# A Strassen-tiled decoder kernel: when the first weight sums of a wide phase are loaded, and in which order its side work runs

## The chip, the cores and the metric

The kernel runs on one core of one Trainium2 chip. The metric is the device time of one execution in microseconds; a profile of one execution gives the time of each instruction.

## The reference

Two decoder layers on 256 tokens of width 2048, in fp32. Each layer has a token mixer (layer 0: dilated sliding-window attention; layer 1: stick-breaking attention; both beside a cross-attention into 256 memory tokens) and a gated MLP. The change is in the MLP alone:

```python
def _conv_ffn(h, w_up, w_conv, b_conv, w_down):
    u = h @ w_up                                  # (256 x 2048) @ (2048 x 11264)
    gate, val = jnp.split(u, 2, axis=-1)          # 5632 columns each
    gp = jnp.pad(gate, ((0, 0), (CONV_WIDTH - 1, 0), (0, 0)))
    acc = b_conv + gp[:, CONV_WIDTH - 1:CONV_WIDTH - 1 + S] * w_conv[CONV_WIDTH - 1]
    for j in range(CONV_WIDTH - 1):
        acc = acc + gp[:, j:j + S] * w_conv[j]
    return (jax.nn.silu(acc) * val) @ w_down
```

## The kernel before, in words

Matmuls keep fp32's precision by splitting each operand into a rounded high part and the rest (`split`, L592 to L594: a cast on ScalarE at L593, a difference on VectorE at L594) and adding three products, high by high, low by high, high by low (`mm3`, L127).

**The groups.** The 5632 columns of the MLP are 11 groups of 512. Odd groups (1, 3, 5, 7, 9) are wide: `wide` (L596) forms a group's gate and value columns by a Strassen scheme, seven products in place of eight, in eight units over the 2048 inputs. Even groups are narrow: eight tiles of 128 columns (two pairs, each with gate and value), each a plain product over the 2048 inputs. Narrow group 0 runs alone (`narrow`, L801). The others run beside a wide group (`beside`, L815): each of the eight units of a wide phase has one narrow tile at its side (`ws_beside`, L151), so that a phase makes wide group g and narrow group g + 1. Behind a phase `downs` (L737) multiplies two finished groups by their rows of w_down, in four chunks of 512 output columns, two chunks at a time, eight pieces of weights in all; each chunk's partial result is copied out (L748) and stored or added to memory by a DMA from POOL (L750, L752). So each layer has five wide phases: the first behind narrow(0), four behind downs.

**A unit.** On PE, in this order: the first half of the side tile (16 matmuls, L156), wide products 1, 2, 3 (L127), the side tile's second half, wide products 7, 5, 6, 4. Products 1 to 3 use plain weights, 7 and 5 the first sum d, 6 and 4 the second sum e. The sum d of two quarter blocks comes by DMA: a load on SP (L628) and an accumulating DMA on POOL (L629), written for the first two units ahead of the phase (`first_sums`, L625) and for unit u + 2 within unit u. VectorE then adds twice (L636, L637) for e. Both sums are split into one set of buffers, `forms` (named x in the profile), which the next unit may overwrite only when products 7, 5, 6, 4 are done.

**The side tile.** It takes one of four "s" banks of PSUM; the other three are held by wide products, so the next side tile can begin only when the last one has been copied (L168, ScalarE) and added (L169, VectorE) out of its bank. Its weights are split in two halves into "whi" and "wlo", four buffers each, shared with the plain weights.

**The pair's steps.** When a pair of side tiles has its gate, the gate is scaled (`gate`, L797), convolved (ScalarE's first tap with the bias at L773, VectorE's other taps at L763, SiLU at L765), and when the value is there multiplied by it (`keep`) and split. These are put in a list (`behind_this`), and `catch_up` takes one entry from it at two places of each unit. The sums of h that products 3, 5, 6, 7 need are made eight in number by `sums_of_h` (L568): five during narrow(0), and the last three from the same list, in the first phase of a layer (L582 to L587, then a split at L285, L286).

**What sets the order.** A planner places instructions by the program's order as far as buffers and its estimates of readiness allow, and each engine then runs its own list in order. Inside a phase the compute instructions are pinned (`pin`): on each engine they stand in the program's order. DMAs are not pinned, nor is anything ahead of the phase's loop or in the downs. "sh" is a pool of 11 buffers for the activations (two for each group), output copies, d and e; "raw" has three buffers for weights as loaded.

Of the kernel before, what the change touches and what calls it, by code (L numbers as in the profile page):

```python
# [10 lines left out]
F32 = mybir.dt.float32  # L11
F32R = mybir.dt.float32r
# [5 lines left out]
P = 128  # L18
# [27 lines left out]
class Body:  # L46
# [103 lines left out]

    def ws_beside(self, out, src, h, done=None):  # L151

        parts = self.piece(src)
        yield
        b = self.bank("s")
        mm = lambda *o, **k: self.pin(self.nc.tensor.matmul(*o, **k))  # L156
# [11 lines left out]
        self.pin(self.nc.scalar.copy(out, b[:, S:]))  # L168
        self.pin(self.nc.vector.tensor_add(out, b[:, 0:S], out))  # L169
        if done:  # L170
            done()
# [396 lines left out]
    def sums_of_h(self, h):  # L568

        nc, pin = self.nc, self.pin
        s = self.sb.tile([P, KT // 2, 4, 2, P], F32R, name="h1", tag="h1", bufs=1)

        def less(out, x, y):

            pin(nc.vector.scalar_tensor_tensor(out, x, -1.0, y, op0=ALU.mult, op1=ALU.subtract))

        def make(i):
            a, d = self.pairtile(), self.pairtile().rearrange("p a (b t) -> p (a b) t", b=2)  # L580
            hh = h[2][:, 2 * i:2 * i + 2, :, :].bitcast(F32)
            pin(nc.vector.tensor_add(a, hh[:, :, 0, :], hh[:, :, 1, :]))  # L582
# [10 lines left out]
        self.pin(self.nc.scalar.copy(hi, of))  # L593
        self.pin(self.nc.vector.tensor_sub(lo, of, hi.bitcast(F32)))  # L594

    def wide(self, src, h, s, forms, r, beside):  # L596

# [24 lines left out]
            nc.sync.dma_start(raw[:, :1536], src[u][:, :1536])  # L622
            return raw

        def first_sums(u):  # L625

            d = self.sh([P, 1024])
            nc.sync.dma_start(d, src[u][:, 512:1536])  # L628
            nc.gpsimd.dma_start(d.rearrange("p (a n) -> p a n", a=2),  # L629
                                src[u][:, 1536:].unsqueeze(1).to_broadcast([P, 2, 512]), accum_op=ALU.add)  # L630
            return d

        def sums(d, raw):

            e = self.sh([P, 1024])
# [14 lines left out]
            for of, parts in zip(t, summed):  # L650
                self.split(*parts, of)

        ahead = [first_sums(0), first_sums(1)]
        raw = load(0)
        t = sums(ahead.pop(0), raw)
        split_sums(t)
        b = beside[0]()
        next(b)
        f = plain(raw)
        self.pinned = True  # L660
        for u in range(n):
            more = u + 1 < n
            next(b)
            if u:
                split_sums(t)
            self.catch_up()
            fa, fb = f
            product(1, u, fa, 1)
            product(2, u, fa, 0)
            product(3, u, fb, 0)  # L670
            if more:
                raw = load(u + 1)
                if u + 2 < n:
                    ahead.append(first_sums(u + 2))
# [32 lines left out]
    def ffn(self, layer, h, each, filler=None, done=None, late=None):  # L707
# [20 lines left out]
        s, make = self.sums_of_h(h)  # L728
        self.later(1, rms)
        for i in range(5):  # L730
            self.later(i + 2, lambda i=i: make(i))
# [3 lines left out]
        acts = {}  # L735

        def downs(groups):  # L737

            lhs = [p for b in groups for p in acts[b]]
            for c0 in (0, 2):  # L740
                banks = {c: [self.bank(), self.bank()] for c in (c0, c0 + 1)}
                for pi, b in enumerate(groups):
                    for c in banks:
                        self.as_piece(banks[c], dn[c, b:], lhs, pi, at=0)
                        if pi == 1:
                            y = self.sh([P, 1024])
                            for t in range(2):
                                nc.scalar.copy(y[:, t * 512:(t + 1) * 512], banks[c][t])  # L748
                            if 0 in groups:
                                nc.gpsimd.dma_start(yout[c], y)  # L750
                            else:
                                nc.gpsimd.dma_start(yout[c], y, accum_op=ALU.add)  # L752

        def conv(p, ga):

            pin, c = self.pin, self.pairtile()

            def shifted():
                for j in range(2):
                    w = weights(2 * p + j)  # L760
                    for i in (1, 0):
                        d = 2 - i
                        pin(nc.vector.scalar_tensor_tensor(c[:, j, d:], ga[:, j, :S - d], w[i], c[:, j, d:],  # L763
                                                           op0=ALU.mult, op1=ALU.add))
                pin(nc.scalar.activation(c, c, AF.Silu))  # L765
# [5 lines left out]
            for j in range(2):  # L771
                w = weights(2 * p + j)
                pin(nc.scalar.activation(c[:, j, :], ga[:, j, :], AF.Identity, scale=w[2], bias=w[3]))  # L773
            return c, shifted

        def weights(ft):
            return [self.cols[:, cv + i * NFT + ft:cv + i * NFT + ft + 1] for i in range(4)]

        def keep(p, c, val):

            g, o = p // 2, p % 2 * 2
            self.pin(nc.vector.tensor_tensor(c, c, val, op=ALU.mult))

            def parts():
                if g not in acts:
                    acts[g] = []
                    room[g] = self.sh([P, 4, S], F32R), self.sh([P, 4, S], F32R)
                hi, lo = room[g]
                self.split_heads(c, hi[:, o:o + 2, :], lo[:, o:o + 2, :])
# [10 lines left out]

        def narrow(g):  # L801
            for p in (2 * g, 2 * g + 1):
                w = place(p)
                ga = self.ws_pair(up[w, 0], h)
                if p == 0:

                    val = self.ws_pair(up[w, 1], h)
                gate(ga)
                c, shifted = conv(p, ga)
                shifted()  # L810
                if p:
                    val = self.ws_pair(up[w, 1], h)
                keep(p, c, val)()

        def beside(g):  # L815

# [2 lines left out]
            def tile(p, i, j):  # L819
# [1 line left out]
                    st[p] = [self.pairtile() for _ in range(2)]  # L821
                ga, val = st[p]

                def first():
                    gate(ga)
                    st["c"], st["shifted"] = conv(p, ga)

                def product():
                    st["parts"] = keep(p, st["c"], val)

                done = None
                if j == 1:
                    done = (lambda: self.behind_this(first, lambda: st["shifted"]())) if i == 0 else (
                        lambda: self.behind_this(product, lambda: st["parts"]()))
                return self.ws_beside(st[p][i][:, j, :], up[place(p), i][j], h, done)
# [4 lines left out]
        def turned(g, made, i):  # L840

            both = []
            for of, sign in zip(made, (1.0, -1.0)):
# [7 lines left out]
            c, shifted = conv(2 * g + i, both[0])  # L851
            shifted()
            keep(2 * g + i, c, both[1])()

        narrow(0)
        self.behind_this(*(lambda i=i: make(i) for i in range(5, KT // 2)))
        forms = self.sb.tile([P, 4, 1024], F32R, name="x", tag="x", bufs=1)
        for g in WIDE:
            made = self.wide(uw[WIDE.index(g)], h, s, forms, R[0], beside(g + 1))
# [304 lines left out]
```

## Time and profile before

| | us |
|---|---|
| median of 3 runs | 2408.19 (2407.2 to 2410.14) |
| the profiled execution | 2404.74 |
| its span in the profile | 2403.0 |
| PE / VectorE / ScalarE busy | 2249.9 / 1657.3 / 1302.3 |
| mean granted TensorE clock | 0.969 |

The span runs from the first to the last instruction; busy is the union of an engine's instructions. Rows of the trace are: start in us from the span's start, us, engine, line, operation, output<-inputs, count; in square brackets the engine's idle time ahead of it and what ended it.

### The profile page before, as it was taken

How to read it: one execution, taken by the hardware profiler on the slowest of the kernel's cores; microseconds unless marked ns; L12 is line 12 of the kernel's file. 1: busy time of each engine (PE TensorE's matmuls, PEld its weight loads, DVE VectorE, ACT ScalarE, POOL GpSimd, SP SyncE). 2: the span in 40 equal slices, each digit the busy share in tenths (PEclk: the TensorE clock that was granted, in tenths of full speed). 3: DMA queues.
4: the chain of work that ended last, by engine and by line, in shares of the span. 5: the costliest groups of instructions: out<-in, count | busy, mean ns of one | idle time of the engine just before them, and what ended most of it. 6: DMA issues, size and time to landing. Idle time of an engine off the chain costs nothing.

```text
span 2403.0 us, 29033 instructions
## 1 busy us (share of the span) xinstructions
PE 2249.9 (94%) x10962; PEld 1867.8 (78%) x10962; DVE 1657.3 (69%) x2175; ACT 1302.3 (54%) x1844; POOL 148.6 (6%) x168
## 2 busy tenths in 40 slices
PE   9999999898997989979999999998989979899798
PEld 7888888676776767767888888886777767677676
DVE  6567668875766757657774667588757667576676
ACT  7556556554554545545664554565555545455454
POOL 0000000001001010010000000000010010100101
PEclk9999999998998989989999999999999989899899
DMA  8745556867759688596745445657587696876964
GB/s 320 255 162 193 170 200 209 234 201 241 228 176 263 199 237 235 184 253 213 283 170 193 155 161 173 230 177 230 190 250 237 183 263 201 238 236 185 258 237 179
DMA packets 102381, 516.79 MB, mean 215 GB/s; under 512 B 10464, under 2 KB 10848, under 8 KB 61920
## 3 DMA queue, kind: packets, MB, share of 16 engines
q1 hardware_dynamic: 72288, 439.43, 52.4%
q0 software_dynamic: 29952, 75.51, 15.5%
q8 instruction: 86, 1.41, 0.2%
q14 instruction: 55, 0.45, 0.1%
HBM read 491.82 MB, written 23.07 MB: 214 GB/s over the span
## 4 chain that ended last, share of the span: by engine, by line
PE 82%; DMA 7%; DVE 6%; issue 3%; ACT 2%; SPq 0%; DVEq 0%; POOL 0%; POOLq 0%; ACTq 0%
PE ps_g L127 35%; PE ps_s L156 18%; PE ps_g L144 11%; PE ps_s L127 8%; DMA sh<-in_uw_dram 6%; PE ps_g L145 6%; DVE wlo L594 3%; ACT whi L593 1%; PE ps_s L848 1%; PE ps_g L147 1%; PE ps_s L272 1%; DVE qk L169 1%; DVE qk L763 1%; DMA raw<-in_up_dram 0%; DVE x L594 0%
## 5 line engine op out<-in xcount | busy, mean ns | idle before, releaser
L594 DVE TENSOR_TENSOR wlo<-raw,whi 128x1024 fp32r<-128x1024 f32 (+1 forms) x758 | 870.2, 1164 | 506.4 <-ACT whi L593 488.3
L593 ACT CAST whi<-raw 128x1024 fp32r<-128x1024 f32 (+1 forms) x758 | 752.4, 1001 | 590.2 <-PE ps_s L156 248.6
L156 PE MATMUL ps_s<-h,whi 128*128 128x512 f32 x1280 | 495.7, 421 | 77.1 <-DVE qk L169 77.0
L127 PE MATMUL ps_g<-whi,sh 128*128 128x512 f32 x1488 | 464.3, 393 | 0.0
L144 PE MATMUL ps_g<-h,whi 128*128 128x512 f32 x1200 | 430.7, 401 | 0.2 <-DVE h L262 0.2
L156 PEld LDWEIGHTS ps_s<-h,whi 128*128 128x128 f32 x1280 | 254.5, 199 | 161.9 <-DVE qk L169 106.5
L156 PE MATMUL ps_s<-h,wlo 128*128 128x256 f32 x1280 | 359.9, 291 | 3.1 <-DVE wlo L594 3.1
L145 PE MATMUL ps_g<-h,wlo 128*128 128x256 f32 x1280 | 346.3, 281 | 0.0
L127 PEld LDWEIGHTS ps_g<-whi,sh 128*128 128x128 f32 x1488 | 277.8, 188 | 57.6
L127 PE MATMUL ps_g<-wlo,sh 128*128 128x512 f32 x744 | 291.9, 392 | 0.0
L127 PE MATMUL ps_g<-whi,h 128*128 128x512 f32 x880 | 276.4, 395 | 1.2 <-ACT whi L593 1.2
L144 PEld LDWEIGHTS ps_g<-h,whi 128*128 128x128 f32 x1200 | 225.5, 188 | 51.5 <-DVE h L262 0.7
L156 PEld LDWEIGHTS ps_s<-h,wlo 128*128 128x128 f32 x1280 | 256.2, 200 | 11.4 <-DVE wlo L594 4.0
L145 PEld LDWEIGHTS ps_g<-h,wlo 128*128 128x128 f32 x1280 | 241.9, 189 | 6.3
L593 ACT CAST x<-sh 128x1024 fp32r<-128x1024 f32 x160 | 165.5, 1048 | 99.6 <-DMA sh<-in_uw_dram 67.8
L127 PE MATMUL ps_g<-x,h 128*128 128x512 f32 x480 | 151.1, 422 | 58.1 <-ACT x L593 55.7
L594 DVE TENSOR_TENSOR x<-sh,x 128x1024 fp32r<-128x1024 f32 x160 | 189.2, 1219 | 0.2 <-ACT x L593 0.2
L127 PEld LDWEIGHTS ps_g<-whi,h 128*128 128x128 f32 x880 | 160.4, 190 | 35.5 <-ACT whi L593 2.1
L127 PE MATMUL ps_g<-wlo,h 128*128 128x512 f32 x440 | 172.8, 393 | 0.6 <-DVE wlo L594 0.5
L127 PEld LDWEIGHTS ps_g<-wlo,sh 128*128 128x128 f32 x744 | 139.8, 188 | 32.0
L127 PEld LDWEIGHTS ps_g<-x,h 128*128 128x128 f32 x480 | 95.5, 201 | 83.9 <-ACT x L593 58.2
L127 PE MATMUL ps_s<-x,h 128*128 128x512 f32 x480 | 144.3, 411 | 0.0
(180 smaller groups left out, 2038.6 us busy)
## 6 DMA issues: line engine op xcount, KB each, us to landing
raw<-in_up_dram SPq DMA_DIRECT2D x96, 1024.0 KB, 5.3
raw<-in_dn_dram SPq DMA_DIRECT2D x88, 1024.0 KB, 4.9
raw<-in_uw_dram SPq DMA_DIRECT2D x80, 768.0 KB, 5.9
sh<-in_uw_dram SPq DMA_DIRECT2D x80, 512.0 KB, 7.4
sh<-in_uw_dram POOLq DMA_DIRECT2D x80, 512.0 KB, 7.2
raw<-in_wqk_a_dram SPq DMA_DIRECT2D x24, 1024.0 KB, 4.8
yout<-sh POOLq DMA_DIRECT2D x32, 512.0 KB, 8.7
raw<-in_wo_b_dram SPq DMA_DIRECT2D x16, 1024.0 KB, 5.0
```

The source lines that it names most:

```text
L127: mm = lambda *o, **k: self.pin(self.nc.tensor.matmul(*o, **k))
L144: mm(b, whi[:, ks], both, start=kt == 0, stop=False)
L145: mm(b[:, 0:S], wlo[:, ks], one, start=False, stop=False)
L147: mm(b, whi[:, ks], both, start=False, stop=True)
L156: mm = lambda *o, **k: self.pin(self.nc.tensor.matmul(*o, **k))
L169: self.pin(self.nc.vector.tensor_add(out, b[:, 0:S], out))
L272: self.nc.tensor.transpose(b[:, k * S + t * P:k * S + (t + 1) * P], self.x[:, t, kt * P:(kt + 1) * P], self.ident)
L593: self.pin(self.nc.scalar.copy(hi, of))
L594: self.pin(self.nc.vector.tensor_sub(lo, of, hi.bitcast(F32)))
L763: pin(nc.vector.scalar_tensor_tensor(c[:, j, d:], ga[:, j, :S - d], w[i], c[:, j, d:], op0=ALU.mult, op1=ALU.add))
L848: nc.tensor.transpose(b[:, j * S + t * P:j * S + (t + 1) * P], of[t][:, f:f + P], self.ident)
```

## The change

Three edits:

1. `first_sums` becomes a method; it is called for a phase's units 0 and 1 half way through the downs that stand ahead of the phase, behind the first two chunks (`early`), and for a layer's first phase within `narrow(0)`, ahead of its second pair. `wide` gets the two tiles as `ahead`.
2. The side tile's weights are split in two steps. In a unit the next tile's first half is split, then this tile's second products and its sum (L168, L169) follow, and then the next tile's second half is split. Before, both halves were split ahead of the sum.
3. The list of a pair's steps is cut finer: gate, ScalarE's taps, VectorE's taps, SiLU, and product, high part, low part, each an entry of its own. The last three sums of h are split one entry later than they are made.

```diff
     def ws_beside(self, out, src, h, done=None):
-        parts = self.piece(src)
-        yield
+        raw = self.sb.tile([P, 2048], F32, name="raw", tag="raw", bufs=3)
+        self.nc.sync.dma_start(raw, src)
+        parts = []
+        for i in range(2):
+            parts.append([self.sb.tile([P, 1024], F32R, name=k, tag=k, bufs=4) for k in ("whi", "wlo")])
+            self.split(*parts[i], raw[:, i * 1024:(i + 1) * 1024])
+            yield
...
-            self.split_heads(d, s[:, i, :, 0, :], s[:, i, :, 1, :])
+            return lambda: self.split_heads(d, s[:, i, :, 0, :], s[:, i, :, 1, :])
...
-    def wide(self, src, h, s, forms, r, beside):
+    def first_sums(self, src, u):
+        d = self.sh([P, 1024])
+        self.nc.sync.dma_start(d, src[u][:, 512:1536])
+        self.nc.gpsimd.dma_start(d.rearrange("p (a n) -> p a n", a=2),
+                                 src[u][:, 1536:].unsqueeze(1).to_broadcast([P, 2, 512]), accum_op=ALU.add)
+        return d
+
+    def wide(self, src, ahead, h, s, forms, r, beside):
...
-        ahead = [first_sums(0), first_sums(1)]
         raw = load(0)
         t = sums(ahead.pop(0), raw)
         split_sums(t)
         b = beside[0]()
         next(b)
+        next(b)
         f = plain(raw)
...
             self.catch_up()
-            next(b)
             if more:
                 after = beside[u + 1]()
                 next(after)
+            next(b)
             next(b, None)
+            if more:
+                next(after)
             product(7, u, summed[0], 1)
...
+        def early(i):
+            ahead[:] = [self.first_sums(uw[i], u) for u in range(2)]
...
                                 nc.gpsimd.dma_start(yout[c], y, accum_op=ALU.add)
+                if c0 == 0:
+                    early(WIDE.index(groups[1] + 1))
...
-            return c, shifted
+            return c, (straight, shifted, silu)
...
-            return parts
+            return product, high, low
...
             for p in (2 * g, 2 * g + 1):
+                if p % 2:
+                    early(0)
                 w = place(p)
...
+                def done():
+                    if i == 0:
+                        st["c"], steps = conv(p, ga)
+                        self.behind_this(lambda: gate(ga), *steps)
+                    else:
+                        self.behind_this(*keep(p, st["c"], val))
...
-        self.behind_this(*(lambda i=i: make(i) for i in range(5, KT // 2)))
+        made = []
+
+        def rest(i):
+            if made:
+                made.pop()()
+            if i < KT // 2:
+                made.append(make(i))
+
+        self.behind_this(*(lambda i=i: rest(i) for i in range(5, KT // 2 + 1)))
```

`straight`, `shifted` and `silu` are the three parts of the convolution, `product`, `high` and `low` those of `keep`; outside a wide phase they are called one behind the other as before.

More of the change, by code (lines that the diff above doesn't have):

```diff
@@ L752, in downs, with weights, straight @@
                                 nc.gpsimd.dma_start(yout[c], y, accum_op=ALU.add)
+                if c0 == 0:
+                    early(WIDE.index(groups[1] + 1))
+        def weights(ft):
+            return [self.cols[:, cv + i * NFT + ft:cv + i * NFT + ft + 1] for i in range(4)]
         def conv(p, ga):
             pin, c = self.pin, self.pairtile()
+            def straight():
+                for j in range(2):
+                    w = weights(2 * p + j)
+                    pin(nc.scalar.activation(c[:, j, :], ga[:, j, :], AF.Identity, scale=w[2], bias=w[3]))
             def shifted():
@@ L769, in shifted, with product, high @@
                         nc.scalar.preload_act_table_set("natural_log_exp_and_others"))
-            for j in range(2):
-                w = weights(2 * p + j)
-                pin(nc.scalar.activation(c[:, j, :], ga[:, j, :], AF.Identity, scale=w[2], bias=w[3]))
-            return c, shifted
-        def weights(ft):
-            return [self.cols[:, cv + i * NFT + ft:cv + i * NFT + ft + 1] for i in range(4)]
+            return c, (straight, shifted, silu)
         def keep(p, c, val):
             g, o = p // 2, p % 2 * 2
-            self.pin(nc.vector.tensor_tensor(c, c, val, op=ALU.mult))
-            def parts():
+            part = lambda i: room[g][i][:, o:o + 2, :]
+            def product():
+                self.pin(nc.vector.tensor_tensor(c, c, val, op=ALU.mult))
+            def high():
                 if g not in acts:
@@ L787, in parts, with low, at_once @@
                     room[g] = self.sh([P, 4, S], F32R), self.sh([P, 4, S], F32R)
+                self.pin(nc.scalar.copy(part(0), c))
+            def low():
+                self.pin(nc.vector.tensor_sub(part(1), c, part(0).bitcast(F32)))
                 hi, lo = room[g]
-                self.split_heads(c, hi[:, o:o + 2, :], lo[:, o:o + 2, :])
                 acts[g] += [(hi[:, o + j, :], lo[:, o + j, :]) for j in range(2)]
-            return parts
+            return product, high, low
+        def at_once(steps):
+            for step in steps:
+                step()
         room = {}
@@ L822, in tile @@
                 ga, val = st[p]
[L824 to L835, printed above, removed]
+                def done():
[4 more added lines that the diff above has]
+                        self.behind_this(*keep(p, st["c"], val))
+                return self.ws_beside(st[p][i][:, j, :], up[place(p), i][j], h, done if j else None)
             return [lambda p=p, i=i, j=j: tile(p, i, j)
```

27 lines of the change are left out of this document (11 added, 16 removed).

## The prediction

> **What bounds the kernel now.** The page comes first: it says which engine sets the end.
>
> ```profile
> span 2403.0 us, 29033 instructions
> PE 2249.9 (94%) x10962; PEld 1867.8 (78%) x10962; DVE 1657.3 (69%) x2175; ACT 1302.3 (54%) x1844; POOL 148.6 (6%) x168
> PEclk9999999998998989989999999999999989899899
> ```
>
> TensorE is busy 94% of the span, so time can be won only where it idles (2403.0 - 2249.9 = 153.1 us) or runs at a lower granted clock (the 8s). The waits say who holds it: the first two rows are PE's own, the third is VectorE's.
>
> ```profile
> PE ps_s L156 <- DVE qk L169: 77.0, 30, 5.8
> PE ps_g L127 <- ACT x L593: 55.7, 8, 8.1
> DVE sh L636 <- DMA sh<-in_uw_dram: 98.5, 10, 13.3
> ```
>
> The columns are total, times, longest, in us. 132.7 of PE's 153.1 idle us are two waits. Thirty times the side tile (L156) waits until VectorE has added up the previous side tile (L169) and so freed its bank; eight times the wide products (L127) wait for the split of the first weight sums (L593), whose DMA VectorE awaits too (L636). Both belong to the ten wide phases, which I cut out with a table by stage: first and last of the eight phases that follow downs, their sum, then the two that follow a narrow group.
>
> ```profile
> 569.30:676.09 106.79, 93.54 (x425) 76.02 (x424) 73.55 (x88) 53.81 (x68) 10.09 (x9) 0.90 0.79 234
> 2221.37:2326.00 104.63, 89.80 (x425) 72.85 (x424) 73.37 (x88) 53.79 (x68) 10.43 (x9) 0.93 0.82 240
> sum 842.80, PE 727.46 PEld 590.01 DVE 587.52 ACT 430.41 POOL 82.70; mean PE 90.93 PEld 73.75 DVE 73.44 ACT 53.80 POOL 10.34
> 422.47:523.57 101.10, 89.49 (x426) 73.09 (x425) 82.41 (x110) 55.57 (x73) 7.11 (x6) 0.95 0.74 223
> 1623.76:1727.46 103.70, 91.77 (x425) 74.74 (x424) 81.54 (x109) 54.50 (x72) 7.11 (x6) 0.93 0.71 217
> ```
>
> After the width come PE, PE loads, VectorE, ScalarE and POOL busy, then granted clock, DMA share and GB/s. What a phase would take without waits I read in the chain, where each row is the first half of a side tile (16 matmuls):
>
> ```profile
> 2106.91 3.05 PE ps_s L156 x16
> 2119.88 3.05 PE ps_s L156 x16
> 2130.60 3.04 PE ps_s L156 x16
> 2138.55 0.70 PE ps_g L127 x3
> 2141.34 3.05 PE ps_s L156 x16
> 617.25 4.61 PE ps_s L156 x16
> ```
>
> Undisturbed, a unit takes 2141.34 - 2130.60 = 10.74 us; the one from 2106.91 took 12.97, a wait of 2.2 more. Eight clean units are 85.9 us. The eight phases hold 842.8 - 8 x 85.9 = 155.6 us above that: 842.8 - 727.5 = 115.3 idle, and 727.5 - 687.2 = 40.3 of slower matmuls, the clock's share. The two others hold 204.8 - 171.8 = 33.0. So 188.6 us are within reach.
>
> **Part 1: first sums begun half way through the downs.** Removed: the wait at the head of eight phases. Its rows, each from its engine's order of time:
>
> ```profile
> 702.50 0.33 SPq L622 DMA_DIRECT2D raw<-in_uw_dram  x1
> 719.04 1.91 SPq L628 DMA_DIRECT2D sh<-in_uw_dram  x3
> 729.96 1.21 POOL L629 DMA_DIRECT2D sh<-in_uw_dram  x1 [5.94 <-DMA sh<-in_uw_dram]
> 736.66 0.69 DVE L636 TENSOR_TENSOR sh<-sh,raw 128x512 f32<-128x512 f32 x1 [13.34 <-DMA sh<-in_uw_dram]
> 736.65 1.04 ACT L593 CAST x<-sh 128x1024 fp32r<-128x1024 f32 x1 [8.96 <-DMA sh<-in_uw_dram]
> 729.25 0.39 PE L156 MATMUL ps_s<-h,whi 128*128 128x512 f32 x1
> 737.75 0.79 PE L127 MATMUL ps_g<-x,h 128*128 128x512 f32 x1 [8.11 <-ACT x L593]
> raw<-in_uw_dram SPq DMA_DIRECT2D x80, 768.0 KB, 5.9
> sh<-in_uw_dram SPq DMA_DIRECT2D x80, 512.0 KB, 7.4
> sh<-in_uw_dram POOLq DMA_DIRECT2D x80, 512.0 KB, 7.2
> ```
>
> A sum is a load on SP (L628), then an accumulating DMA on POOL (L629). The load went out at 719.04, at the downs' end, though the phase's plain weights, later in the program, went at 702.50: the planner had let them pass, since the 11 "sh" buffers were taken. After the change the two loads come earlier in the program than the last two chunks' output buffers. Half way I count six "sh" buffers for three groups' activations, one for the memory keys (layer 0), two outputs: two are free. The downs run from 676.09 to 721.82, so half way is 699. The sum lands at 699 + 7.4 + 1.2 + 7.2 = 715; two adds (2 x 0.69), the cast 1.04 and its difference (1.2, half of the 2.36 in row 769.00 below) end near 719. PE needs it after the side tile at 729.6: ten microseconds to spare. If that cover went, the 8.1 would come back. The plain weights (702.50 + 5.9) are there at 708, so nothing else is late. Past the moved DMAs SP has the second half's down pieces (2 x 0.4 us of issue), POOL the last two output stores, behind accumulates that await their loads; a store there only frees a buffer. Cost: nothing to 1 us a phase; I take it into the leftover. In the phases behind a narrow group only a little of VectorE's work moves forward.
>
> **Part 2: a tile's sum right behind its products; steps one by one.** Nothing is added, and each engine issues the same instructions. The old order on a unit with a conv step:
>
> ```profile
> 756.03 1.05 ACT L593 CAST whi<-raw 128x1024 fp32r<-128x1024 f32 x1 [1.98 <-PE ps_s L156]
> 765.39 1.92 DVE L763 SCALAR_TENSOR_TENSOR qk<-qk,cols 128x255 f32<-128x255 f32 x4
> 769.00 2.36 DVE L594 TENSOR_TENSOR wlo<-raw,whi 128x1024 fp32r<-128x1024 f32 x2 [1.70 <-ACT whi L593]
> 769.82 0.36 ACT L168 COPY qk<-ps_s 128x256 f32<-128x256 f32 x1
> 771.28 0.42 DVE L169 TENSOR_TENSOR qk<-ps_s,qk 128x256 f32<-128x256 f32 x1
> 771.75 0.50 PE L156 MATMUL ps_s<-h,whi 128*128 128x512 f32 x1 [2.24 <-DVE qk L169]
> ```
>
> VectorE does the conv (1.92), both halves of the next tile's split (2.36), and only then the sum. The new order is: first half of the split, sum, second half. Let T be the end of the side tile's products. Four wide products follow (4 x 0.70), so the bank must be free at T + 2.8. ScalarE's copy (0.36, allowed a start 0.2 us late) and the add (0.42) make T + 1.0: 1.8 us spare. The moved second half (cast, then 1.2 on VectorE) is done near T + 2.9; PE wants it behind the next first half and three products, 2.8 + 3.05 + 3 x 0.70 = T + 7.9. ScalarE now waits for PE at the sum with that cast queued behind, but the cast waited for the same products already (row 756.03). Worst unit, with the conv first: from T, VectorE has add and second half (to 2.9), sums' split 2 x 1.2 held by the last wide product (5.3), conv 1.9 (7.2), adds 1.4 (8.6), plain split 1.2 + 0.6 (10.4), first half 1.2 (11.6), sum 12.1; the bank is due at 10.7 + 2.8 = 13.5. So no wait is next, by 1.4 us. The other steps (gate, ScalarE's conv, SiLU, product, parts) are shorter.
>
> In the phase behind narrow(0), VectorE is the scarce one:
>
> ```profile
> 429.77 0.69 DVE L582 TENSOR_TENSOR qk<-h 128x512 f32<-128x512 f32 x1
> 432.20 0.69 DVE L286 TENSOR_TENSOR h<-qk,h 128x512 fp32r<-128x512 f32 x1 [0.69 <-ACT h L285]
> 438.30 0.69 DVE L286 TENSOR_TENSOR h<-qk,h 128x512 fp32r<-128x512 f32 x1 [0.68 <-ACT h L285]
> 441.53 0.42 DVE L169 TENSOR_TENSOR qk<-ps_s,qk 128x256 f32<-128x256 f32 x1
> 442.00 0.80 PE L156 MATMUL ps_s<-h,whi 128*128 128x512 f32 x1 [5.02 <-DVE qk L169]
> ```
>
> Between 429.77 and 441.94 lie two makes of h's sums, each with 0.7 us of waiting for ScalarE. With the split one step later both waits, one difference (0.7) and half a tile's split (1.2) leave the chain: 3.3 us, 1.7 of 5.0 left. The same two phases' later waits go as above, but VectorE's 82.4 busy us leave little air under 85.9. I put these phases at 92 us each, bounds 87 and 97.
>
> **The clock.** Row 617.25 shows a first half at 4.61 instead of 3.05 us behind a wait of 2.2, so short waits cost clock too, sometimes; all of the 40.3 us hang on waits that go. The Trainium skill, "TensorE: Matmul & The Clock Gate", section "Why this matters for your kernels", puts the harmful gap above some 3 us; this row differs. By the page the 1.56 us of such a row would stay; I count seven of them behind the twenty short waits, 11 us, and the forecast would be 2259.
>
> **The sum.** Eight phases: 155.6, less a leftover of 2 us each (bounds 0 and 5) = 139.6. Two phases: 204.8 - 2 x 92 = 20.8. Together 160.4 of the profiled execution's 2404.74 us gives 2244.3; the median of the runs is 3.45 above it, so 2248. With the low bounds: 155.6 + 30.8 = 186.4, 2222. With the high ones: 115.6 + 10.8 = 126.4, 2282.
>
> **Rivals.** *The DMA engines become the bound.*
>
> ```profile
> 720.00:760.00 40.00, 28.92 (x122) 22.78 (x121) 20.62 (x24) 16.23 (x19) 6.86 (x6) 0.83 0.99 268
> 760.00:800.00 40.00, 37.75 (x190) 31.00 (x189) 32.70 (x40) 22.48 (x28) 3.57 (x3) 1.00 0.81 241
> ```
>
> These 80 us move 20.4 MB, 2.1 of them the two sums that go ahead. The rest at 268 GB/s needs 68 us, while the forecast leaves about 60.5. Buffers filled ahead should absorb that. If they don't, 7.5 us a phase return, 8 x 7.5 = 60: 2308. The Trainium skill, "DMA: Bandwidth & Descriptors", section "Issuing engines are not separate DMA queues", speaks for this one: the earlier loads share the engines with the downs' pieces; the share of 0.99 agrees.
>
> *Only the order within the unit works*, because the planner again lets the plain weights pass the sums (the row at 702.50 shows it can). Then 16 waits of 2.25, five slow halves of 1.56 and 20.8 go: 64.6, 2344.
>
> *VectorE is held in the downs, and it gets slower.* It works in order. If the planner counts on an earlier landing than the chip gives and puts the adds ahead of a down piece's split, the 13.3 us of row 736.66 return where PE has only the pieces already split. Adds ahead of the sixth piece (due five eighths through the downs, at 704.7) and the sum at 715, add and split done at 717.6: PE waits 13 us with its tail of clock, still less than the 17.5 saved. It decides beyond that; with the sum landing 10 us later, at 725, the downs lose 24.5, 7 more than is saved: 56 - 20.8 = +35, 2443. Against it: the downs' pieces come first in the program, and the sums have no short load time to be mistaken by 20 us.
>
> **How the numbers follow.** Forecast 0.74, DMA bound 0.13, half of it 0.08, held VectorE 0.05 (slower in most of that). The range runs from the low bound with 4 us for what I overlooked, 2218, to the DMA rival, 2308; beyond it lie the last two and the tails. A measurement tells about 0.2% from no change, so faster 0.94, same 0.01, slower 0.05.
>
> **What would show it.** Right: L628 before 705 in a downs such as this one, no PE wait for x by L593, under five waits for L169, all in the phases behind narrow(0); granted clock above 0.98 in the eight phases, each 86 to 89 us; downs unchanged at 45.5. DMA bound: VectorE's waits for in_uw or ScalarE's for in_up within units 0 to 5. Held VectorE: PE idle in the downs behind wlo. I am wrong if waits for L169 stay in units 2 and 6, or the slow matmuls stay without waits.

## The result, and the profile after

The changed kernel takes 2291.15 us (median of 4 runs, 2287.66 to 2292.92), the kernel before 2409.16 us on the same chip: a ratio of 0.950 [0.948, 0.953]. The forecast was 2248 us, with a range of 2218 to 2308 us: the time lies inside the range, 43 us above the forecast. The profiled execution took 2287.66 us. Of all executions told of here two ran at a lower granted clock and are in no ratio: one of four of "after, sums at the start" in the table below (2394 us), and one of the kernel before, beside two of the later kernels (3153 us). From the page after: the span, TensorE's line and the granted clock in 40 slices.

```profile
span 2285.9 us, 28964 instructions
PE 2212.9 (97%) x10962; PEld 1853.1 (81%) x10962; DVE 1659.3 (73%) x2175; ACT 1304.1 (57%) x1844; POOL 149.4 (7%) x168
PEclk9999999999999999999999999999999999999999
```

The 8s are gone, and PE's idle time went from 153.1 to 2285.9 - 2212.9 = 73.0 us. The waits of PE (total, times, longest), where lines have moved: the side tile is L162, its sum L175, the split L600 (cast) and L601 (difference), the first sums L606 and L607.

```profile
PE ps_s L162 <- DVE qk L175: 31.4, 10, 5.2
PE ps_g L127 <- ACT whi L600: 20.3, 9, 3.0
PE ps_g L127 <- DVE wlo L601: 5.5, 9, 0.7
```

The waits for the tile's sum fell from 77.0 us in thirty to 31.4 in ten, and the waits for the split x, 55.7 us, are no longer there. New is the second row: wide products that wait for whi, the cast of a raw piece. A table by stage says where that is. First the wide phases (the first behind narrow(0), two behind downs, the last of all, and the sum of all ten), then the first two of the eight downs and the sum of these, and last the same sum in the kernel before; columns as in the prediction.

```profile
422.38:513.00 90.62, 86.31 (x425) 71.79 (x424) 82.00 (x109) 55.38 (x73) 7.11 (x6) 0.98 0.81 247
558.72:645.48 86.76, 84.17 (x425) 70.66 (x424) 71.42 (x85) 52.80 (x67) 7.76 (x7) 1.00 0.85 264
696.35:784.94 88.59, 85.79 (x426) 71.94 (x424) 71.47 (x85) 52.82 (x67) 8.03 (x7) 0.98 0.85 259
2117.43:2208.69 91.26, 86.11 (x425) 72.28 (x424) 71.46 (x85) 52.90 (x67) 8.03 (x7) 0.96 0.83 252
sum 892.54, PE 857.09 PEld 717.44 DVE 735.95 ACT 533.76 POOL 77.97; mean PE 85.71 PEld 71.74 DVE 73.59 ACT 53.38 POOL 7.80
513.00:558.72 45.72, 45.72 (x209) 37.72 (x208) 30.79 (x38) 27.16 (x38) 4.17 (x5) 1.00 0.71 235
645.48:696.35 50.87, 47.87 (x209) 38.70 (x208) 30.69 (x38) 27.03 (x38) 5.05 (x5) 0.97 0.72 210
sum 402.95, PE 379.89 PEld 307.89 DVE 245.67 ACT 216.43 POOL 38.81; mean PE 47.49 PEld 38.49 DVE 30.71 ACT 27.05 POOL 4.85
sum 365.83, PE 365.83 PEld 301.93 DVE 228.25 ACT 209.13 POOL 19.03; mean PE 45.73 PEld 37.74 DVE 28.53 ACT 26.14 POOL 2.38
```

The ten phases fell from 842.8 + 204.8 = 1047.6 to 892.5 us: 155.1 won, where the forecast had 160.4. The eight downs grew from 365.8 to 403.0 us: 37.2 lost, where it had nothing. All else went from 989.5 to 990.4. So 155.1 - 37.2 - 0.9 = 117.0 of the 117.1 us by which the span fell. The largest miss is in the downs: the first is as long as before, the other seven are 3.1 to 6.2 us longer. Of the 37.2 us, 23.1 are waits of PE (403.0 - 379.9, where there were none) and 14.1 slower matmuls (379.9 - 365.8). The end of the second downs, from the timelines of SP, POOL, ScalarE, VectorE and PE:

```profile
666.04 0.98 SPq L606 DMA_DIRECT2D sh<-in_uw_dram  x2
676.18 1.21 POOL L607 DMA_DIRECT2D sh<-in_uw_dram  x1 [4.21 <-DMA sh<-in_uw_dram]
674.69 1.05 ACT L600 CAST whi<-raw 128x1024 fp32r<-128x1024 f32 x1 [1.70 <-PE ps_g L127]
686.11 1.05 ACT L600 CAST x<-sh 128x1024 fp32r<-128x1024 f32 x1 [10.38 <-DMA sh<-in_uw_dram]
687.07 1.99 ACT L600 CAST whi<-raw 128x1024 fp32r<-128x1024 f32 x2
687.19 1.23 DVE L601 TENSOR_TENSOR x<-sh,x 128x1024 fp32r<-128x1024 f32 x1 [10.20 <-ACT x L600]
688.34 4.62 DVE L601 TENSOR_TENSOR wlo<-raw,whi 128x1024 fp32r<-128x1024 f32 x4
685.47 0.40 PE L127 MATMUL ps_g<-wlo,sh 128*128 128x512 f32 x1
688.16 0.73 PE L127 MATMUL ps_g<-whi,sh 128*128 128x512 f32 x2 [2.29 <-ACT whi L600]
689.61 0.50 PE L127 MATMUL ps_g<-wlo,sh 128*128 128x512 f32 x1 [0.72 <-DVE wlo L601]
```

The loads go out 20.6 us into the downs, and the first sum lands at 686.1, 40.6 us in: nearly as forecast (39). But ScalarE stood idle for 10.38 us before the cast of that sum, x, and only behind it are the casts of the downs' eighth piece (687.07), whose products PE has been ready for since 685.87. The planner has listed the sum's cast ahead of the last down piece's, and on VectorE the sum's difference ahead of that piece's differences. The wait is 2.29 + 0.72 us, and PE's busy time in this downs is 47.87 where the first has 45.72: slower matmuls, with a granted clock of 0.97. In the first downs the order is the same, but the sum lands 35.9 us in (548.85) and PE waits for nothing. Why it lands sooner there stays open: the first downs' output stores don't accumulate, but neither do the fifth's, where the sum lands 40.2 us in (1685.76) and the downs takes 3.1 us longer.

The waits for the tile's sum that are left sit at one place in the eight phases behind downs, between units 1 and 2. The same views a little later:

```profile
693.37 0.42 SPq L606 DMA_DIRECT2D sh<-in_uw_dram  x1
703.60 1.21 POOL L607 DMA_DIRECT2D sh<-in_uw_dram  x1 [5.03 <-DMA sh<-in_uw_dram]
715.63 0.69 DVE L643 TENSOR_TENSOR sh<-sh,raw 128x512 f32<-128x512 f32 x1 [6.50 <-DMA sh<-in_uw_dram]
720.32 0.50 PE L162 MATMUL ps_s<-h,whi 128*128 128x512 f32 x1 [2.80 <-DVE qk L175]
```

The third sum of the phase, unit 2's, is loaded only at the end of the downs and takes 22 us from the load to VectorE's add, where the prediction counted 7.4 + 1.2 + 7.2; VectorE waits 6.5 us for it, and with it the tile's sum queued behind.

### The profile page after: what moved, and what is told of

The parts are those of the page before. It is cut to its first block, busy times and chain, and to the rows that moved or that the text cites. A ratio compares the mean times of both kernels' runs of the same rounds, so it can differ in the third digit from the quotient of the medians.

```text
span 2285.9 us, 28964 instructions
## 1 busy us (share of the span) xinstructions
PE 2212.9 (97%) x10962; PEld 1853.1 (81%) x10962; DVE 1659.3 (73%) x2175; ACT 1304.1 (57%) x1844; POOL 149.4 (7%) x168
## 4 chain that ended last, share of the span: by engine, by line
PE 79%; DMA 12%; DVE 4%; issue 2%; ACT 2%; SPq 0%; POOLq 0%; POOL 0%; DVEq 0%; ACTq 0%
PE ps_g L127 30%; PE ps_s L162 18%; DMA sh<-in_uw_dram 11%; PE ps_g L144 11%; PE ps_s L127 9%; PE ps_g L145 6%; DVE wlo L601 2%; ACT whi L600 1%; PE ps_g L147 1%; DMA raw<-in_up_dram 1%; PE ps_s L278 1%; DVE qk L785 1%; DMA raw<-in_wmv_dram 0%; ACT x L600 0%; PE ps_s L874 0%
## 5 line engine op out<-in xcount | busy, mean ns | idle before, releaser
L601 DVE TENSOR_TENSOR wlo<-raw,whi 128x1024 fp32r<-128x1024 f32 (+1 forms) x758 | 868.9, 1164 | 317.1 <-ACT whi L600 311.0
L600 ACT CAST whi<-raw 128x1024 fp32r<-128x1024 f32 (+1 forms) x758 | 757.5, 1004 | 503.2 <-PE ps_g L127 178.4
L162 PE MATMUL ps_s<-h,whi 128*128 128x512 f32 x1280 | 475.3, 406 | 31.4 <-DVE qk L175 31.4
L127 PE MATMUL ps_g<-whi,sh 128*128 128x512 f32 x1488 | 472.2, 399 | 18.6 <-ACT whi L600 18.6
L162 PE MATMUL ps_s<-h,wlo 128*128 128x256 f32 x1280 | 352.4, 286 | 3.0 <-DVE wlo L601 3.0
L162 PEld LDWEIGHTS ps_s<-h,whi 128*128 128x128 f32 x1280 | 247.0, 193 | 92.7 <-DVE qk L175 36.3
L127 PE MATMUL ps_g<-wlo,sh 128*128 128x512 f32 x744 | 296.7, 399 | 4.5 <-DVE wlo L601 4.5
L162 PEld LDWEIGHTS ps_s<-h,wlo 128*128 128x128 f32 x1280 | 248.0, 194 | 14.1 <-DVE wlo L601 3.9
L601 DVE TENSOR_TENSOR x<-sh,x 128x1024 fp32r<-128x1024 f32 x160 | 192.0, 1222 | 79.6 <-ACT x L600 79.6
L600 ACT CAST x<-sh 128x1024 fp32r<-128x1024 f32 x160 | 168.1, 1052 | 111.3 <-DMA sh<-in_uw_dram 89.2
L607 POOL DMA_DIRECT2D sh<-in_uw_dram x80 | 96.0, 1200 | 669.3 <-DMA sh<-in_uw_dram 400.0
L127 PE MATMUL ps_g<-x,h 128*128 128x512 f32 x480 | 137.6, 394 | 0.0
L127 PE MATMUL ps_s<-x,h 128*128 128x512 f32 x480 | 137.2, 394 | 0.0
```

Source lines behind the costliest of these rows:

```text
L607: self.nc.gpsimd.dma_start(d.rearrange("p (a n) -> p a n", a=2), src[u][:, 1536:].unsqueeze(1).to_broadcast([P, 2, 512]), accum_op=ALU.add)
```

## The experiments

Four theories, on the 37 us and on what is left in the phases. **A**: ScalarE stands at the first sum's cast, listed ahead of a down piece's. **B**: the loads half way are too late. **C**: the DMA engines are full, and the loads slow the down pieces. **D**: in the phases, unit 2's sum lands late, because its transfers compete with the first two sums, the stores and the plain weights. After the first four runs D was split: **S**, its load waits for a buffer that the last downs free, and **J**, its transfers are slowed by others. All times are medians; phases, downs and rest are of the profiled execution, in us; each ratio is to runs of the kernel before on the same chip.

| kernel | ten phases | eight downs | rest | span | median | ratio to before [95%] |
|---|---|---|---|---|---|---|
| before | 1047.6 | 365.8 | 989.5 | 2403.0 | 2409.2 | 1 |
| after | 892.5 | 403.0 | 990.4 | 2285.9 | 2291.2 | 0.950 [0.948, 0.953] |
| order alone | 953.4 | 365.8 | 989.9 | 2309.1 | 2312.5 | 0.960 [0.957, 0.962] |
| tile's sum alone | 991.3 | 365.8 | 992.0 | 2349.1 | 2350.0 | 0.975 [0.973, 0.978] |
| steps alone | 987.5 | 365.8 | 988.4 | 2341.7 | 2343.1 | 0.973 [0.969, 0.976] |
| early sums alone | 970.6 | 402.6 | 988.8 | 2361.9 | 2367.7 | 0.983 [0.980, 0.986] |
| after, sums at the start | 889.5 | 365.8 | 991.1 | 2246.3 | 2248.6 | 0.932 [0.929, 0.935] |
| after, casts behind | 923.7 | 365.8 | 992.6 | 2282.1 | 2282.1 | 0.947 [0.944, 0.949] |
| both of these | 886.3 | 365.8 | 989.8 | 2241.9 | 2242.4 | 0.931 [0.928, 0.933] |
| both, plain stores | 864.9 | 365.8 | 992.0 | 2222.7 | 2221.3 | 0.922 [0.919, 0.924] |
| casts behind, three sums half way | 881.1 | 366.9 | 989.6 | 2237.5 | 2239.3 | 0.929 [0.927, 0.931] |
| both, three sums | 856.3 | 367.1 | 991.4 | 2214.8 | 2218.9 | 0.921 [0.919, 0.923] |

**Order alone.** The kernel after, with the first two sums begun at the phase's head again.

```diff
@@ wide
+        ahead = [self.first_sums(src, u) for u in range(2)]
         raw = load(0)
@@ downs, narrow
-                if c0 == 0:
-                    early(WIDE.index(groups[1] + 1))
-                if p % 2:
-                    early(0)
```

> Edits 2 and 3 alone: the first sums of units 0 and 1 are loaded at the phase's head again, as before. If the two parts act on their own, the eight waits of about 7 us for the first sum stay, the sixteen waits of 2.25 us for the tile's sum go, and the downs stay at 45.7 us each: 2344 us, the sum of the prediction's second rival. If the order within the unit does nothing, 2408. If it is the order within the unit that disturbs the downs, these rise to 50 us here too.

Measured 2312.5 us, and PE's waits are

```profile
PE ps_g L127 <- ACT x L600: 57.0, 8, 8.3
PE ps_s L162 <- DVE qk L175: 17.3, 10, 2.3
```

and its eight phases behind downs, summed:

```profile
sum 773.85, PE 701.25 PEld 578.90 DVE 590.49 ACT 433.43 POOL 82.69; mean PE 87.66 PEld 72.36 DVE 73.81 ACT 54.18 POOL 10.34
```

The order by itself takes some 97 us off and leaves the eight head waits whole; the downs are 45.7 us each. So the early sums, put on top, bring only 21 us more (23 in the profiled executions: 61 in the phases, less 37 in the downs).

**The order in halves, and the early sums alone.** Three kernels made from the one before: the raw load in two pieces with the tile's sum right behind its products; the steps one by one; the early sums.

```diff
@@ tile's sum alone: ws_beside, wide
-        parts = self.piece(src)
-        yield
+        raw = self.sb.tile([P, 2048], F32, name="raw", tag="raw", bufs=3)
+        self.nc.sync.dma_start(raw, src)
+        parts = []
+        for i in range(2):
+            parts.append([...])
+            self.split(*parts[i], raw[:, i * 1024:(i + 1) * 1024])
+            yield
... (the hunks of next(b) and next(after) in wide, as in the change)
@@ steps alone: the hunks of conv, keep, beside, make and rest, without those above
@@ early sums alone: the hunks of first_sums and early, without those of the order
```

> The kernel before with one half of the order alone: the raw load split in two pieces and a tile's sum right behind its products, the pair's steps still in the two lumps of before, the first sums still begun at the phase's head. The whole order alone took 96.6 us off (2312.5). Theory T (the order of the tile's sum is what counts: VectorE's copy and add stood behind a cast pair): the thirty waits for the sum, 77 us, fall to under 25 us, and the total is 2315 to 2340 us. Theory L (the lump of a pair's steps is what holds VectorE: six taps in a row ahead of the copy): under 30 us of the 97 are won, the waits for the sum stay above 50 us, and the total is 2380 to 2409 us.

> The kernel before with the other half of the order alone: a pair's steps and the sums of h one by one, the tile's sum where it stood before, the first sums at the phase's head. The whole order took 97 us off, the tile's sum alone 60. If the two halves add (theory T+L), this one takes 37 us off: 2373 us, with some 55 us of the thirty waits for the sum left. If the steps count only where the tile's sum already stands right behind its products (theory Q: the sum is queued behind what stands ahead of it, lump or steps), the waits stay at 70 to 80 us and the total at 2395 to 2410 us.

> The kernel before with the first part of the change alone: the first two sums of a phase begun half way through the downs, the order within the units as it was. Theory A (ScalarE stands at the first sum's cast, listed ahead of the last down piece's): the eight waits of a phase's first product for x, 55.7 us, go, and the downs grow from 45.7 to some 50.4 us as in the kernel after, for those 37 us; the phases keep the thirty waits for the tile's sum, 77 us. The kernel after less the order alone is 61 us fewer in the phases, so by addition 2409 - 61 + 37 = 2385 us. Rival: the order of before holds VectorE at the phase's start, so that the early sum isn't used and a wait of the same length comes at unit 0's end; phases within 20 us of the 1047.6 and the downs still longer, 2425 to 2446 us.

PE's waits of the three, in this order:

```profile
PE ps_g L127 <- ACT x L598: 58.0, 8, 8.1
PE ps_s L161 <- DVE qk L174: 45.4, 30, 3.9
```

```profile
PE ps_g L127 <- ACT x L595: 58.1, 8, 8.2
PE ps_s L157 <- DVE qk L170: 27.7, 11, 4.1
```

```profile
PE ps_s L156 <- DVE qk L169: 82.6, 30, 5.8
PE ps_g L127 <- ACT whi L593: 17.5, 7, 3.0
PE ps_g L127 <- DVE wlo L594: 3.0, 8, 0.7
```

The tile's sum alone takes 60 us off, the steps alone 67, both together 97: neither T nor L nor Q. Each half by itself shortens what VectorE has ahead of the tile's sum. With the sum first, the thirty waits stay but shrink, most of them to 1.3 us; with the steps apart, nineteen of thirty vanish. The early sums alone take 42 us off, 17 more than by addition: they win 77 us in the phases and lose the same 37 in the downs, with the same wait for whi. So that loss belongs to the early sums and not to the order.

**The sums at the start of the downs; the casts behind.** Two ways to cure the downs. The first calls `early` ahead of the loop over the chunks. The second leaves the loads where they are and holds the adds and splits of unit 0's sums back until the downs' last split has been issued on ScalarE and on VectorE.

```diff
@@ sums at the start: downs
             lhs = [p for b in groups for p in acts[b]]
+            early(WIDE.index(groups[1] + 1))
             for c0 in (0, 2):
...
-                if c0 == 0:
-                    early(WIDE.index(groups[1] + 1))
@@ casts behind: split, wide
+        self.last_split = (self.pin(self.nc.scalar.copy(hi, of)),
+                           self.pin(self.nc.vector.tensor_sub(lo, of, hi.bitcast(F32))))
...
-        t = sums(ahead.pop(0), raw)
-        split_sums(t)
+        act, dve = (i.ins for i in self.last_split)
+        with self.tc.issue_after(act), self.tc.issue_after(dve):
             t = sums(ahead.pop(0), raw)
             split_sums(t)
```

> The changed kernel with the two early loads put at the start of the downs, some 23 us sooner. Theory A (the wait in the downs is ScalarE standing at the cast of the first sum, which the planner lists ahead of a down piece's casts because it reckons with an earlier landing): the cast moves forward with the load and stands ahead of a piece near the downs' beginning, so the wait stays and only changes its place, 5 to 9 us in each of seven downs, 2285 to 2330 us. Theory B (the load merely starts too late for the downs): earlier is enough, the downs return to 45.7 us, 2254.

> The changed kernel; loads where they are, but the adds, casts and differences of unit 0's sums are queued behind the casts and differences of the last down piece. Theory A: downs back to 45.7 us, 37 us less than the changed kernel, 2254; the waits for the tile's sum between units 1 and 2 (2.6 to 5.2 us) stay. Theory B and a third, C (the down pieces are late because the 16 DMA engines are shared): the wait in the downs stays, 2291.

> Both edits: loads at the start of the downs, and the work on the first sums queued behind the last down piece. Theory A: downs at 45.7 us, no wait for the first sums. Theory D on the waits between units 1 and 2 (unit 2's accumulate lands late because it competes with the first two sums, the outputs' stores and the plain weights at the downs' end): with the first two sums out of the way these waits shrink from about 3 us to under 1, and with their tails of clock some 15 to 25 us go: 2230 to 2240. If they have another cause, 2254 as with the casts queued alone.

Casts behind: the downs are 45.7 us each again, with loads and transfers as in the kernel after. That is theory A, and it speaks against C: the same transfers cost the downs nothing. But only 9 of the 37 us arrive (4 in the profiled executions: the phases take 31 us more). From this kernel, PE's largest waits, SP's loads at the downs' end (the first is unit 2's), and VectorE's add for unit 2 in the second phase (690.40 to 782.54):

```profile
PE ps_s L162 <- DVE qk L175: 51.6, 11, 7.3
690.49 7.48 SPq L606 DMA_DIRECT2D sh<-in_uw_dram  x2
713.45 0.69 DVE L643 TENSOR_TENSOR sh<-sh,raw 128x512 f32<-128x512 f32 x1 [9.56 <-DMA sh<-in_uw_dram]
```

The phase starts 5.95 us earlier than in the kernel after (696.35), but unit 2's sum is there only 2.2 us earlier (715.63): most of the time won is given back there. That is the late sum of theory D, which hid behind the first loss; what makes it late is taken up below.

Sums at the start: A expected the wait to stay, since the casts are listed as before. It doesn't. The planner issued the loads earlier still, some 20 us ahead of the downs (which begin at 642.75), and the cast has nothing to wait for:

```profile
622.20 0.90 SPq L606 DMA_DIRECT2D sh<-in_uw_dram  x2
642.96 1.07 ACT L600 CAST x<-sh 128x1024 fp32r<-128x1024 f32 x1
```

A's forecast of 2285 to 2330 us missed and B's number is right: 2248.6 us. What A says of the mechanism is not refuted, since the cast still comes first and the sum is just there. With both edits, 2242.4 us, and the waits for the tile's sum stay, 27.4 us in ten, eight of them between units 1 and 2. D had these below 1 us with the sums at the start: that cause falls, at least as the only one.

**Three sums, and plain stores.** On top of both edits: three sums begun ahead instead of two; or, for the other, every store of a downs' result a plain one, which leaves out the accumulation over a layer's downs.

```diff
@@ three sums: early, wide
-            ahead[:] = [self.first_sums(uw[i], u) for u in range(2)]
+            ahead[:] = [self.first_sums(uw[i], u) for u in range(3)]
-                if u + 2 < n:
-                    ahead.append(self.first_sums(src, u + 2))
+                if u + 3 < n:
+                    ahead.append(self.first_sums(src, u + 3))
@@ plain stores: downs
-                                nc.gpsimd.dma_start(yout[c], y, accum_op=ALU.add)
+                                nc.gpsimd.dma_start(yout[c], y)
```

> The loads at the start of the downs, the casts behind its last split, and three first sums there instead of two, unit u+3's being begun in unit u. What is left in e9 are ten waits for DVE's L175, 27.4 us, nearly all between units 1 and 2, where DVE's add for unit 2 waits for the second sum. Theory S (unit 2's load waits for a buffer that the last down piece frees, then 12 us for the accumulation): the sum that was begun at the start of the downs is there, those waits go in the eight phases behind downs, which fall from 88.4 to some 85.3 us, and the total from 2242 to about 2217 us. Theory J (the 16 DMA engines are full at the phase's start, and whichever sum is loaded there comes late): the wait only moves to the next sum, unit 3's, or to the downs, whose pieces' raw loads then come late; 2235 to 2250 us.

> As e9 (loads at the start of the downs, casts behind its last split), with every store of a downs' result a plain one, so that nothing is accumulated over the downs of a layer: the output lacks all downs but the last of each layer. Everything else is issued as in e9. Theory J: the accumulating stores of the third and fourth chunk, still under way when unit 2's sum is loaded, are what makes that sum late; the six phases behind accumulating downs fall to the 85.3 us of the two behind plain ones, and the total from 2242 to about 2222 us. Theory S (the late buffer): the load is issued no earlier, and the total stays within 6 us of 2242 us.

Three sums: 2218.9 us, S's number. PE's waits, and two of its phases:

```profile
PE ps_s L162 <- DVE qk L175: 6.7, 5, 3.1
PE ps_s L162 <- DVE wlo L601: 5.1, 2, 3.6
557.60:641.55 83.95, 83.95 (x426) 70.77 (x424) 71.84 (x85) 52.70 (x67) 10.09 (x9) 1.00 0.92 284
687.29:771.36 84.07, 84.07 (x426) 70.68 (x425) 72.01 (x86) 53.15 (x67) 10.42 (x9) 1.00 0.94 291
```

The eight phases behind downs take 84 to 84.8 us with PE busy throughout and the clock at 1.00; a clean unit is 83.95 / 8 = 10.49 us. What is left is in the two phases behind narrow(0), 89.4 and 93.1. This is the fastest kernel of the study, 3.2% below the changed one (2218.9 / 2291.2).

Plain stores: 2221.3 us, J's number. From "both" (phase from 687.90), unit 2's load on SP and VectorE's add; the same from this kernel (phase from 688.89), with the matmul behind it; then the median from issue to landing of these stores, in "both" and in this kernel:

```profile
685.09 0.42 SPq L606 DMA_DIRECT2D sh<-in_uw_dram  x1
707.14 0.69 DVE L643 TENSOR_TENSOR sh<-sh,raw 128x512 f32<-128x512 f32 x1 [6.51 <-DMA sh<-in_uw_dram]
```

```profile
686.08 0.45 SPq L606 DMA_DIRECT2D sh<-in_uw_dram  x1
706.11 0.69 DVE L643 TENSOR_TENSOR sh<-sh,raw 128x512 f32<-128x512 f32 x1 [4.49 <-DMA sh<-in_uw_dram]
710.79 0.50 PE L162 MATMUL ps_s<-h,whi 128*128 128x512 f32 x1 [0.79 <-DVE qk L175]
```

```profile
yout<-sh POOLq DMA_DIRECT2D x32, 512.0 KB, 8.5
```

```profile
yout<-sh POOLq DMA_DIRECT2D x32, 512.0 KB, 6.5
```

The load leaves 2.8 us ahead of the phase in both, but with plain stores the sum is there 17.2 us into the phase and not 19.2, and PE's wait is 0.79 us in place of 2.80: here the transfers are faster, and the load no earlier. So S and J are not rivals. Unit 2's sum is late by some 3 us; a load issued earlier removes that, and so do plain stores. Neither is shown to be the only cause.

**Casts behind, three sums half way.** The smallest mend of the change as it stands: loads half way, the two edits "casts behind" and "three sums".

> The kernel after with two edits: the first units' adds and casts behind the downs' last split, and three first sums begun half way through the downs instead of two; the loads stay half way. Theories A and S: the downs are back at 45.7 us, unit 2's sum is begun early enough, the waits between units 1 and 2 go, and the total is that of the kernel with three sums at the start of the downs, 2215 to 2228 us. Theory J (three accumulations in the second half of the downs, beside the accumulating stores and the last pieces' raw loads, come as late as the two did at the phase's start): one of the three sums is late by 3 us or more in a phase, or the downs' last pieces are; 2240 to 2285 us.

Measured 2239.3 us, 0.7 us below J's range and 11 us above the end of A and S's. The two phases behind plain-store downs are clean (83.95), the others 86.6 to 90.2. In the second phase (688.27 to 778.03), ScalarE waits for the side tile's raw weights:

```profile
698.31 1.05 ACT L600 CAST whi<-raw 128x1024 fp32r<-128x1024 f32 x1 [3.04 <-DMA raw<-in_up_dram]
```

Their load is issued at 690.41, 2.1 us behind the phase's start, where "both, three sums" issues it 1.0 us ahead (686.26), and it takes about as long (7.8 and 7.3 us). SP had waited 5.7 us for VectorE to empty a buffer, which stood behind the first sum's split; that sum had landed at 685.49, 12.5 us after its accumulation was issued. VectorE too sits idle for 3.57 us up to 698.23, for which the profile shows no cause, so how much of the loss is the weights' stays open. With three sums, the loads half way cost 20 us against the start of the downs (2239.3 and 2218.9).

## Why the prediction was right, and where it was not

**The number.** 2291 us lies above 2282 us, the forecast's sum with its high bounds. It is inside the range because the range was drawn out to the DMA rival's 2308 us, and the loss that filled this room came in the downs, in another way: that the range held is in part luck. With the downs cured by the loads at the start, the phases win 158 us against the forecast's 160.4, and the time is 2248.6 us.

**Part 2 held.** The order removed what it was to remove: the sixteen waits in units 2 and 6 are gone. The second rival priced this part alone at 2344 us and it gave 2312: the chain of steps was right, and its worth understated. Most of the difference lies in the eight phases: they fell by 69.0 us (842.8 to 773.85), 42.7 in shorter waits, where 36 was counted, and 26.2 in faster matmuls, where 7.8 was counted. The phases behind narrow(0) fell to 89.5 and 90.0, 25.3 us against 20.8.

**Part 1 held in the phases.** The loads left 20.6 us into a downs, the sum landed 40.6 in, and no product waits for x at the phase's head. Eight phases: 842.8 - 712.6 = 130.2 won against 139.6; two phases: 204.8 - 180.0 = 24.8 against 20.8 (90.6 and 89.4 instead of 92). The leftover was 89.07 - 85.9 = 3.2 us a phase instead of 2, with one wait in each for unit 2's sum, whose load the prediction had not followed. Its clean unit, 10.74 us, was itself 0.25 too long, as the kernel with three sums shows: above that kernel's 83.95 us the leftover is 5.1.

**The step that failed** is "so nothing else is late", with its price "nothing to 1 us a phase". It followed the moved DMAs past SP's and POOL's queues, and not their first consumer on ScalarE. The cast of the sum belongs to the phase, but once its load was begun in the downs, the planner placed it ahead of the last piece's casts; why it did so is not shown. The sum landed within 2 us of the forecast and ten ahead of the phase's start, and that was still later than the downs' need of the engine that stood waiting. Measured: 37.2 us in eight downs, where the sum had 0 to 8; with the casts queued behind the last piece they are gone from the downs.

**The third rival** named this mechanism, "held in the downs", with 13 to 24.5 us a downs instead of 4.7, and gave it a chance of 0.05 because "the downs' pieces come first in the program". The order in which ScalarE ran its casts shows that the program's order did not bind the planner there. VectorE was held too, as it said, but not by the adds: it stood at the sum's difference, behind ScalarE's cast, and its adds came behind the last piece. The price was smaller: the cast stood ahead of the eighth piece only, not of the sixth. Its direction, slower than before, was wrong.

**The DMA engines** were not the bound: the two phases of 84 us shown above moved 284 and 291 GB/s, more than the 268 that the rival took for the limit. But single transfers came late, which is what remained, and the sign set for this rival showed in part: in the kernel after VectorE waits for in_uw twenty times, 68.6 us in all, 6.5 of them at 715.63.

**The signs.** Forecast: under five waits for the tile's sum, all behind narrow(0); measured ten, eight of them behind downs. Clock above 0.98 in eight phases: between 0.96 and 1.00. Each of them 86 to 89 us: 86.8 to 91.3. Downs unchanged: wrong, which is the sign that should have been worked out in the sum.

## What to carry to other kernels

When a transfer is moved ahead, follow its consumer too: a compute step whose input is loaded earlier may be listed earlier on an engine that works in order, and then it blocks work that is more urgent, for as long as the transfer is still under way. Begin it early enough that it has landed by the first place where its consumer can be listed, or tie the consumer behind the urgent work. And after mending one wait, look for the next with a fixed time of its own: casts behind won 37 us in the downs and gave 31 back in the phases until the third sum was begun ahead as well.

## What the runs showed of the hardware

Waits of about 2 us can cost clock. In "casts behind, three sums half way", after waits of 0.65, 0.28 and 2.17 us within 14 us (the last ends at 702.91):

```profile
698.77:704.00 5.23, 3.06 (x15) 2.21 (x14) 5.20 (x8) 3.70 (x5) 0.56 (x1) 0.99 1.03 335
704.00:710.00 6.00, 6.00 (x24) 5.06 (x23) 5.04 (x6) 2.26 (x3) 1.84 (x2) 0.72 1.03 386
```

The granted clock is 0.72 over these 6 us, with PE busy throughout; in a window from 703.90 to 707.30 it is 0.50. Not every such wait costs it: behind one of 2.59 us in the kernel after, it is 1.00 from 582.43 to 588.43. The Trainium skill, "TensorE: Matmul & The Clock Gate", section "Why this matters for your kernels", puts the harmful gap above some 3 us; the drop measured here came without one, as the row in the prediction did.

An accumulating transfer of 512 KB from POOL took between 6.0 and 13.5 us from issue to landing in the kernel after, with a median of 9.4 (7.2 in the kernel before); the one issued at 703.60 was awaited until 715.63, 12.0 us. No run here shows one alone. The Trainium skill, "DMA: Bandwidth & Descriptors", section "Anatomy of one DMA — SWDGE (gpsimd) path", gives a fit of 2.0 us and the bytes at 436 GB/s, an estimate of 3.2 us for 512 KB; that section has no accumulation in it, and even the shortest measured here is nearly twice that.
